# One test behind the output in place of two in the MoE; residual and first gate as identity products, second gate by token tiles

## The chip, the cores and the metric

The kernel runs on one core of one Trainium2 chip. The metric is the device time of the whole program in microseconds (us); lower is better. Before the change the median of three runs is 1718.18 us (1717.43 to 1719.94). Besides, one execution was recorded by the hardware profiler; all rows below are from it. The engines are called PE (TensorE; PEld is its weight load), DVE (VectorE), ACT (ScalarE), POOL (GpSimd) and SP (SyncE, which here issues the transfers).

## The reference

Four transformer layers run on 256 tokens of width 1024, in float32: two layers of a first kind (a mixer of three attentions, then a mixture of experts) and two of a second kind (a mixer of three branches, then a feed-forward). The change touches the mixture of experts of the first kind:

```
for i in range(2):
    ...                                                       # mixers
    h = layer_norm(ALPHA * h + mix, ln1_g[i], ln1_b[i])
    ffn = grouped_moe(h, ...)                                 # 16 experts, each token picks 2
    ple = sigmoid(h @ ple_gate[i]) * (p[i] @ ple_proj[i])
    h = layer_norm(ALPHA * h + ffn + ple, ln2_g[i], ln2_b[i])
```

`grouped_moe` gives each token two experts of one group with weights that add up to one; an expert computes `silu(h @ w_gate) * (h @ w_up) @ w_down` with 512 hidden columns.

## The kernel before

The program is first recorded as a list of operations in program order; `order` then plays a model of the engines, of the transfers and of the buffers, and writes out, for each engine, an order by earliest start, and among those that can start by place in the list (`prio`, which `prefer` and `arrange` change). Every operation is issued by one line, 554 (`call`), so groups in the profile are told apart by tile names. Engines work through their own order and wait for one another by semaphores.

Work is split into two tiles `t` of 128 tokens and column halves `n` of 512. Weights come by SP in blocks of up to 512 KB (`chunk`). Outside the experts each block `raw` is split by ACT and DVE into a high and a low part (`whi`, `wlo`) and multiplied in three passes with the split activations. Expert weights (`deep`) are used as they are, in plain fp32. `raw`, `deep`, `whi`, `wlo`, the activations `x`, `h` and the tile `r` share 43 large buffers (`big`); 128x512 work tiles share ten (`t2k`); PSUM has eight banks (`ps`).

In `moe`, a layer's mixture of experts is computed with 64 slots per expert. `r` is first set to twice the scaled residual; `ple` for the first column half multiplies the gate (`pg`) and the projection (`pp`) and adds the product to `r`. `route` picks the experts and numbers the tokens of each; `slot` is a token's place in its expert, `most` the largest number of tokens of one expert. `gather` forms the expert inputs (`xg`) by one-hot products. Then eight pairs `q` of experts follow: `gate_up` (tile `gu`), `hidden`, `down` (tiles `yh`, `yl`), and `scatter`, which adds the outputs of the pair to four PSUM banks `acc[n, t]`. In the last pair (`PLE_AT`), `ple` of the second half stands between the gate/up products and the down products, for both token tiles.

After the last scatter stands a branch: every engine loads `most` (line 561) and compares (line 562); if an expert had more than 64 tokens, `moe_rest` runs all experts densely for the tokens left over and adds to `r`. The branch has `scratch` tiles, and no operation that touches `r`, `x` or these tiles is moved across it. Then `layernorm` adds `r` at 0.5 to `acc` (`lnt`), takes the statistics, normalizes half by half and hands each half to `feat`, which transposes it (`fT`) and splits it into the next `x`. The work on the next layer's weights (`whi`, `wlo`) may start before that. At the very end SP writes the two halves of the output and waits for them.

Of the kernel before, what the change touches and what calls it, by code (L numbers as in the profile page):

```python
# [17 lines left out]
L = 2  # L18
S = 256
# [262 lines left out]
class Op:  # L282
    __slots__ = ("i", "eng", "fn", "args", "kw", "dur", "lat", "deps", "users", "new", "tiles", "epoch", "wait", "prio", "table", "cols", "body", "mode",
# [11 lines left out]
class Pool:  # L295
# [3 lines left out]
    def tile(self, shape, dtype, name, tag=None, bufs=None, cls=None):  # L299
        if self.rec.sink is not None:  # L300
            return next(self.rec.scratch[cls if cls in self.rec.scratch else tag]).bitcast(dtype)
# [6 lines left out]
BIAS_FIRST = False  # L308
MASK_GP = 0
PLE_AT = (None, 7)  # L310
# [10 lines left out]
class Recorder:  # L321


    def __init__(self, tc):
        self.tc, self.ops, self.bufs, self.sink, self.key = tc, [], {}, None, ()
        self.tensor, self.vector, self.scalar, self.gpsimd, self.sync = (
            Engine(self, n) for n in ("tensor", "vector", "scalar", "gpsimd", "sync"))

    def add(self, eng, fn, args, kw):
        if self.sink is not None:  # L330
            kw.pop("after", None)
            kw.pop("behind", None)
            self.sink.append((eng, fn, args, kw))
            return
        o = Op()
        o.i, o.eng, o.fn, o.args, o.kw, o.body = len(self.ops), eng, fn, args, kw, None
# [23 lines left out]
    def link(self, o, ins, outs):  # L360
        deps, o.tiles = set(), []
        for views, w in ((ins, False), (outs, True)):
            for v in views:
                t = v.t
                if t not in o.tiles:
# [12 lines left out]

    def branch(self, value, limit, body, scratch, behind=()):

        o = Op()
        o.i, o.eng, o.fn, o.args, o.kw = len(self.ops), "branch", "if", (value, limit), {}
        self.sink, self.scratch = [], {v[0].t.cls or v[0].t.tag: itertools.cycle(v) for v in scratch}
        body()
        o.body, self.sink = self.sink, None
        ins = [value] + [x for _, _, a, k in o.body for x in list(a) + list(k.values()) if isinstance(x, V)]
        outs = [x for _, _, a, k in o.body for x in a[:1] if isinstance(x, V)]
        self.link(o, ins, outs)
        o.deps |= set(behind)
        o.dur, o.lat, o.prio, o.nbytes, o.cols, o.table, o.mode = 2200.0, 0.0, o.i, 0, 0.0, (), None  # L390
        self.ops.append(o)


    def order(self):
# [23 lines left out]
        ready = {e: [] for e in ENGINES + ("branch",)}  # L418
# [57 lines left out]
        while len(seq) < len(ops):  # L476
# [35 lines left out]
            if o.eng == "branch":  # L512
                table = None
                for e in clock:
# [1386 lines left out]
```

## Time and profile before

| | us |
|---|---|
| median of 3 runs | 1718.18 |
| profiled execution | 1713.75 |
| its span, first to last instruction | 1711.7 |
| PE busy | 1645.6 (96%) |
| DVE busy | 902.0 (53%) |
| ACT busy | 676.2 (40%) |
| PE matmuls / DVE instructions | 8884 / 1608 |
| mean granted PE clock | 0.987 |

The span runs from the first to the last instruction; the profiled execution's own time has 2.05 us more. A busy share is that of an engine over the whole span. Waits are given as "waiting operation <- what ended the wait: us in total, times, longest". In the timeline a row is a run of equal instructions with its start and length; `x4` is their number, and what stands in brackets is the idle time before it. The MoE of layer 0 ends at about 416 us, that of layer 1 at about 810.

### The profile page before, as it was taken

The page shows a single profiled execution, that of the slowest core. Times are in us where ns is not written, and L with a number is a line of the kernel's source. Part 1 is how long each engine was busy: PE and PEld are TensorE (multiplying, and loading weights), DVE is VectorE, ACT ScalarE, POOL GpSimd, SP SyncE. Part 2 cuts the span into 40 slices and gives each one's busy share as a digit, 9 for nine tenths or more (in the row PEclk, how much of TensorE's full clock was granted, in tenths as well). Part 3 has the DMA queues.
Part 4 walks back from the last instruction along what each step waited for, and adds up shares of the span by engine and source line. Part 5 has one row for each costly group of instructions (what it writes and reads, how often), then busy time and mean ns, then how long its engine had stood idle before and what let it go on. Part 6 is the DMA issues. An engine that isn't in the chain of part 4 may idle for free.

```text
span 1711.7 us, 23099 instructions
## 1 busy us (share of the span) xinstructions
PE 1645.6 (96%) x8884; PEld 1218.5 (71%) x8884; DVE 902.0 (53%) x1608; ACT 676.2 (40%) x1032; POOL 13.0 (1%) x29
## 2 busy tenths in 40 slices
PE   6999999997999999998799999999999999999997
PEld 5887444434798544434697888899989888888996
DVE  7867211014958411103876447955587654785554
ACT  5454111113555211113454554444445454444441
POOL 1000000000000000000000000000000000000000
PEclk9999999999999999999899999999999999999999
DMA  6764899999564799999553347555645334846530
GB/s 220 272 240 153 316 409 409 409 410 371 178 233 163 275 409 409 409 409 405 205 178 132 115 159 272 196 191 185 203 157 197 127 120 148 286 171 207 193 115 25
DMA packets 117297, 414.21 MB, mean 242 GB/s; under 512 B 13250, under 2 KB 15586, under 8 KB 117172
## 3 DMA queue, kind: packets, MB, share of 16 engines
q1 hardware_dynamic: 116580, 411.35, 65.8%
q8 instruction: 73, 1.20, 0.3%
q0 software_dynamic: 592, 1.25, 0.3%
q14 instruction: 52, 0.43, 0.1%
HBM read 410.44 MB, written 2.10 MB: 241 GB/s over the span
## 4 chain that ended last, share of the span: by engine, by line
PE 49%; DVE 2%; issue 0%; ACT 0%; DVEq 0%
PE f L554 11%; PE ff L554 10%; PE gl L554 8%; PE br L554 4%; PE acc L554 3%; PE gv L554 2%; PE gq L554 1%; PE gk L554 1%; PE gg L554 1%; PE mk L554 1%; PE mv L554 1%; PE mq L554 1%; PE fT L554 1%; PE o L554 1%; PE gu L554 1%; DVE wlo L554 0%
## 5 line engine op out<-in xcount | busy, mean ns | idle before, releaser
L554 DVE TENSOR_TENSOR wlo<-raw,whi 128x1024 fp32r<-128x1024 f32 (+1 forms) x370 | 433.6, 1207 | 181.4 <-ACT whi L554 149.8
L554 ACT CAST whi<-raw 128x1024 fp32r<-128x1024 f32 (+1 forms) x370 | 369.1, 1041 | 140.7 <-PE br L554 29.0
L554 PE MATMUL gu<-deep,xg 128*64 128x512 f32 x1024 | 246.9, 597 | 4.9 <-DMA deep<-in_w_up_dram 4.5
L554 PEld LDWEIGHTS gu<-deep,xg 128*64 128x64 f32 x1024 | 76.1, 136 | 157.4 <-issue 126.9
L554 PE MATMUL ff<-whi,f 128*128 128x512 f32 x512 | 137.9, 390 | 0.0
L554 PE MATMUL y<-deep,gu 128*64 128x512 f32 x512 | 122.4, 595 | 1.7 <-DMA deep<-in_w_down_dram 1.4
L554 PE MATMUL f<-x,whi 128*128 128x256 f32 x768 | 123.4, 283 | 0.0
L554 DVE SCALAR_TENSOR_TENSOR yl<-y,gw,yh 128x512 fp32r<-128x512 f32 x32 | 24.0, 751 | 168.8 <-ACT yh L554 168.8
L554 PEld LDWEIGHTS ff<-whi,f 128*128 128x128 f32 x512 | 95.0, 188 | 19.0
L554 PEld LDWEIGHTS f<-x,whi 128*128 128x128 f32 x768 | 106.7, 192 | 0.9
L554 PE MATMUL gl<-whi,x 128*128 128x512 f32 x384 | 104.1, 391 | 0.0
L554 ACT COPY gu<-gu 128x512 f32<-128x512 f32 x32 | 18.7, 585 | 206.9 <-PE gu L554 206.9
L554 PEld LDWEIGHTS y<-deep,gu 128*64 128x64 f32 x512 | 38.9, 137 | 79.9 <-issue 67.5
L554 PEld LDWEIGHTS gl<-whi,x 128*128 128x128 f32 x384 | 71.9, 188 | 14.7
L554 PE MATMUL ff<-wlo,f 128*128 128x512 f32 x256 | 78.9, 389 | 0.0
L554 PE MATMUL f<-x,wlo 128*128 128x256 f32 x384 | 77.4, 283 | 0.0
L554 DVE TENSOR_TENSOR gu<-gu,guT 128x256 f32<-128x256 f32 x32 | 13.3, 420 | 100.8 <-ACT gu L554 100.7
L554 ACT ACTIVATE r<-r 128x512 f32<-128x512 f32 x32 | 20.3, 634 | 111.0 <-DVE r L554 111.0
L554 PE MATMUL gl<-wlo,x 128*128 128x512 f32 x192 | 60.0, 392 | 0.0
L554 PEld LDWEIGHTS f<-x,wlo 128*128 128x128 f32 x384 | 59.9, 192 | 0.0
L554 ACT ACTIVATE yh<-y,gw 128x512 fp32r<-128x512 f32 x32 | 22.0, 687 | 89.8 <-PE y L554 89.8
L554 DVE TENSOR_SCALAR r<-f 128x512 f32<-128x512 f32 x32 | 22.0, 688 | 66.7 <-PE f L554 66.5
(428 smaller groups left out, 2678.2 us busy)
## 6 DMA issues: line engine op xcount, KB each, us to landing
raw<-in_w_in_dram SPq DMA_DIRECT2D x156, 512.0 KB, 4.8
deep<-in_w_gate_dram SPq DMA_DIRECT2D x128, 512.0 KB, 10.2
deep<-in_w_up_dram SPq DMA_DIRECT2D x128, 512.0 KB, 10.2
deep<-in_w_down_dram SPq DMA_DIRECT2D x128, 512.0 KB, 10.2
raw<-in_w_ff_dram SPq DMA_DIRECT2D x128, 512.0 KB, 5.1
raw<-in_w_branch_dram SPq DMA_DIRECT2D x24, 512.0 KB, 4.7
raw<-in_w_o_dram SPq DMA_DIRECT2D x16, 512.0 KB, 5.4
raw<-in_ple_gate_dram SPq DMA_DIRECT2D x16, 512.0 KB, 6.9
```

Source lines behind the costliest of these rows:

```text
L554: getattr(getattr(self.tc.nc, eng), fn)(*[r(a) for a in args], **{k: r(v) for k, v in kw.items()})
```

## The change

The two branches in the MoE go, and `moe_rest` with them. `most` becomes a kept column per layer, and the maximum of both is stored as `many`. Behind the whole program, after the output is issued, one test of `many` follows: if any expert of either layer had more than 64 tokens, the whole program is recorded a second time (`again`) with `moe_all`, which runs all 16 experts densely, and the output is written again.

`r` goes too. The scaled residual, for the first column half together with its gate product, is kept in four 128x512 tiles (`first`) and enters `acc` by products with the identity matrix, fp32, 128x128 by 512 columns, placed in the first pair of experts; the scatters then add to it. `ple` now gives a function `gate_of(t)` for one token tile. For the second half, `gate_of(0)` stands in the last pair where both tiles stood; `gate_of(1)` is recorded after the norm of token tile 0. Its result is added to `acc[1, t]` by DVE. `layernorm` takes its two column halves as they are: `acc[0, t]` directly from PSUM, the other from `second[t]`. For the other norms the sum is now formed by `plus`.

```diff
-    def branch(self, value, limit, body, scratch, behind=()):
...
-    def run(self):
-        seq = self.order()
-        with self.tc.manual_schedule():
-            for o in seq:
-                if o.fn == "if":
-                    n = self.tc.nc.values_load(o.args[0].real(), min_val=0, max_val=S)
-                    with self.tc.If(n > o.args[1]), self.tc.manual_schedule():
-                        for c in o.body:
-                            self.call(*c)
-                else:
-                    self.call(o.eng, o.fn, o.args, o.kw)
+        for o in self.order():
...
+        self.fast = True
+
+    def again(self):
+
+        self.nc = Recorder(self.nc.tc)
+        for p in self.pools:
+            p.rec = self.nc
+        self.fast = False
 
...
-    def layernorm(self, acc, resid, lnp, hnew, x, t, alpha=ALPHA):
+    def plus(self, acc, resid, t, alpha=ALPHA):
+
+        tt = [self.t2k("lnt") for _ in range(2)]
+        for n in range(2):
+            self.nc.vector.scalar_tensor_tensor(tt[n], resid[t][:, n * 512:n * 512 + 512], alpha, acc[n], op0=OP.mult, op1=OP.add)
+        return tt
+
+    def layernorm(self, src, lnp, hnew, x, t):
 
         nc = self.nc
-        tt = [self.t2k("lnt") for _ in range(2)]
         st = self.sm(12, "st")
         for n in range(2):
-            sl = slice(n * 512, n * 512 + 512)
-            nc.vector.scalar_tensor_tensor(tt[n], resid[t][:, sl], alpha, acc[n], op0=OP.mult, op1=OP.add)
-            nc.vector.bn_stats(st[:, n * 6:n * 6 + 6], tt[n])
+            nc.vector.bn_stats(st[:, n * 6:n * 6 + 6], src[n])
         mv = self.sm(2, "mv")
         nc.vector.bn_aggr(mv, st.rearrange("p (a b) -> p a b", b=6))
         rs = self.rsqrt(mv[:, 1:2], 1e-5, 1)
         for n in range(2):
             sl = slice(n * 512, n * 512 + 512)
-            nc.vector.scalar_tensor_tensor(tt[n], tt[n], mv[:, 0:1], lnp[0][:, sl],
-                                           op0=OP.subtract, op1=OP.mult)
-            nc.vector.scalar_tensor_tensor(hnew[t][:, sl], tt[n], rs, lnp[1][:, sl],
-                                           op0=OP.mult, op1=OP.add)
+            tt = self.t2k("lnt") if src[n].t.space == PS else src[n]
+            nc.vector.scalar_tensor_tensor(tt, src[n], mv[:, 0:1], lnp[0][:, sl], op0=OP.subtract, op1=OP.mult)
+            nc.vector.scalar_tensor_tensor(hnew[t][:, sl], tt, rs, lnp[1][:, sl], op0=OP.mult, op1=OP.add)
             if x is not None:
...
+
+    def slots(self, l, pick):
+
+        nc = self.nc
         p = self.ps("pos")
...
-        most = self.small.tile([128, 1], I32, name=self.nm("most"), tag="most", bufs=2)
-        nc.vector.tensor_reduce(most, p[:, 32:48], axis=AX.X, op=OP.max)
-        return gate, slot, most
-
-    def moe_rest(self, l, x, gr, r):
+        nc.vector.tensor_reduce(self.most[:, l:l + 1], p[:, 32:48], axis=AX.X, op=OP.max)
+        if l == L - 1:
+            nc.vector.tensor_reduce(self.many, self.most, axis=AX.X, op=OP.max)
+        return slot
+
+    def moe_all(self, l, h, x):
 
...
-    def ple(self, l, x, px, r, n):
+    def ple(self, l, x, px, n):
 
         nc, A = self.nc, self.A
         wp = self.wblock(A["ple_proj"], l * 256 * D + n * 256 * 512, 2, 512, PLE_CLS)
         pp = []
         for p in self.toks("pp", px, wp):
             a = self.t2k("pp")
-            nc.scalar.copy(a, p)
+            nc.scalar.activation(a, p, AF.Copy, scale=0.5)
             pp.append(a)
         w = self.wblock(A["ple_gate"], l * D * D + n * D * 512, 8, 512, PLE_CLS)
-        for t, p in enumerate(self.toks("pg", x, w)):
+
+        def gate_of(t):
+            p = self.ps("pg", "dense")
+            self.stream((w, [((t,), self.tok(p, x, t))]))
             a = self.t2k("pg")
             nc.scalar.activation(a, p, AF.Tanh, scale=0.5)
             nc.vector.scalar_tensor_tensor(a, a, 1.0, pp[t], op0=OP.add, op1=OP.mult)
-            sl = slice(n * 512, n * 512 + 512)
-            nc.vector.tensor_add(r[t][:, sl], r[t][:, sl], a)
-
-    def moe(self, l, h, x, cap=CAP):
+            return a
+
+        return pp, gate_of
+
+    def moe(self, l, h, x):
+
         nc, A = self.nc, self.A
-        r = self.htile("r")
+        i = len(nc.ops)
+        first = [[], []]
+        _, gate_of = self.ple(l, x, self.load_p(l), 0)
         for t in range(2):
-            nc.scalar.activation(r[t], h[t], AF.Copy, scale=2.0 * ALPHA)
-        i = len(nc.ops)
-        for n in range(2):
-            if PLE_AT[n] is None:
-                self.ple(l, x, self.load_p(l), r, n)
+            a = gate_of(t)
+            nc.vector.scalar_tensor_tensor(a, h[t][:, 0:512], ALPHA, a, op0=OP.mult, op1=OP.add)
+            first[0].append(a)
+            a = self.t2k("ah")
+            nc.scalar.activation(a, h[t][:, 512:1024], AF.Copy, scale=ALPHA)
+            first[1].append(a)
         k = len(nc.ops)
         ht = XT([self.x4("hth", (128, 1024)) for _ in range(2)], [self.x4("htl", (128, 1024)) for _ in range(2)])
         for t in range(2):
             nc.scalar.copy(ht.hi[t], h[t])
             nc.vector.tensor_sub(ht.lo[t], h[t], ht.hi[t])
-        gate, slot, most = self.route(x)
-        gr = self.sm(32, "grest")
-        nc.vector.scalar_tensor_tensor(gr, slot, float(cap), gate, op0=OP.is_gt, op1=OP.mult)
-        if cap < CAP:
-            nc.vector.scalar_tensor_tensor(slot, slot, float(cap), slot, op0=OP.is_le, op1=OP.mult)
+        gate, pick = self.route(x)
+        slot = self.slots(l, pick)
...
-                        nc.tensor.matmul(acc[n, t], ST[q][:, t * 128:(t + 1) * 128], ys[n][i], start=q == 0 and i == 0,
+                        nc.tensor.matmul(acc[n, t], ST[q][:, t * 128:(t + 1) * 128], ys[n][i], start=False,
                                          stop=q == NE // 2 - 1 and i == 1, behind=behind)
...
                 scatter(q - 1, ys, whole)
+            else:
+                for t in range(2):
+                    for n in range(2):
+                        nc.tensor.matmul(acc[n, t], self.ident, first[n][t], start=True, stop=False, behind=whole)
             hid.append(hidden(b[0]))
             if q < 7:
                 a = gate_up(2 * q + 2)[0]
-            for n in range(2):
-                if q == PLE_AT[n]:
-                    self.ple(l, x, self.load_p(l), r, n)
+            else:
+                _, gate_of = self.ple(l, x, self.load_p(l), 1)
+                second = [gate_of(0)]
             ys = down(q, hid)
             if q < 7:
                 b = gate_up(2 * q + 3)
         scatter(7, ys)
-        scratch = [[self.ring_tile("raw")], [self.ring_tile("whi")], [self.ring_tile("wlo")],
-                   [self.t2k("rest") for _ in range(6)], [self.ps("rest") for _ in range(2)]]
-        nc.branch(most[0:1, 0:1], cap, lambda: self.moe_rest(l, x, gr, r), scratch, [len(nc.ops) - 1])
-        return r, acc
-
-    def block1(self, l, h, x, w0=None, cap=CAP):
+
+        def sums(t):
+            if t:
+                second.append(gate_of(t))
+            nc.vector.tensor_add(second[t], second[t], acc[1, t])
+            return acc[0, t], second[t]
+
+        return sums
+
+    def block1(self, l, h, x, w0=None):
         mixT = self.mixers1(l, x, w0)
         hn, x1 = self.wo_ln(l, h, mixT)
-        r, acc = self.moe(l, hn, x1, cap)
+        if self.fast:
+            sums = self.moe(l, hn, x1)
+        else:
+            r = self.moe_all(l, hn, x1)
+            sums = lambda t: [r[t][:, n * 512:n * 512 + 512] for n in range(2)]
         lnp = self.load_lnp(2 * l + 1)
         h2 = self.htile("h2")
         x2 = self.xT("x2")
         for t in range(2):
-            self.layernorm([acc[0, t], acc[1, t]], r, lnp, h2, x2, t, alpha=0.5)
...
         m = Model(tc, A, ctx)
...
+
+        def program():
+            x = m.xT("x")
+            w0 = m.wblock(A["w_in"], 0, 8, W1_BLOCKS[0][1])
+            if m.fast:
+                m.load_bias()
+            for i, c in enumerate(w0):
+                m.load_x(x, i)
+                c()
+            if m.fast:
+                m.setup()
+            h = None
+            for l in range(L):
+                h, x = m.block1(l, h, x, None if l else w0)
+            for l in range(L):
+                h, x = m.block2(l, h, x, l == L - 1)
+            for t in range(2):
+                m.nc.sync.dma_start(out[0, t * 128:(t + 1) * 128], h[t])
+            m.nc.run()
+
+        with tc.manual_schedule():
+            program()
+
+            n = tc.nc.values_load(m.many[0:1, 0:1].real(), min_val=0, max_val=S)
+            with tc.If(n > CAP), tc.manual_schedule():
+                m.again()
+                program()
```

## Rows read from the trace of the kernel before

**Rows 1.** Waits of PE and DVE, 409 to 430, then 805 to 824.
```profile
PE fT L554 <- DVE h L554: 13.1, 1, 13.1
DVE lnt L554 <- DVEq L562: 6.0, 1, 6.0
...
PE fT L554 <- DVE h L554: 12.8, 2, 12.5
DVE lnt L554 <- PEq L562: 5.7, 1, 5.7
```

**Rows 2.** Windows: us, busy PE, PEld, DVE, ACT, POOL, PEclk, DMA share, GB/s.
```profile
416.20:422.80 6.60, 0.01 (x1) 0.00 (x0) 0.64 (x1) 0.90 (x2) 0.00 (x0) 0.76 1.02 391
422.80:429.30 6.50, 0.00 (x0) 0.01 (x1) 6.01 (x17) 2.49 (x4) 0.00 (x0) 0.50 0.28 107
```

**Rows 3.** Timeline, layer 0: start, us, engine, line, operation [idle before].
```profile
401.29 1.07 PE L554 MATMUL pg<-whi,x 128*128 128x512 f32 x4
...
406.82 7.09 PE L554 MATMUL y<-deep,gu 128*64 128x512 f32 x32
...
414.68 0.75 DVE L554 SCALAR_TENSOR_TENSOR yl<-y,gw,yh 128x512 fp32r<-128x512 f32 x1 [0.27 <-ACT yh L554]
...
415.48 0.73 PE L554 MATMUL acc<-yl,oh 128*128 128x512 f32 x2
...
422.84 0.69 DVE L554 SCALAR_TENSOR_TENSOR lnt<-r,acc 128x512 f32<-128x512 f32 x1 [6.00 <-DVEq L562]
...
424.17 0.67 DVE L554 SCALAR_TENSOR_TENSOR lnt<-r,acc 128x512 f32<-128x512 f32 x1
...
429.32 1.09 PE L554 MATMUL fT<-const,h 128*128 128x128 f32 x4 [13.10 <-DVE h L554]
```

**Rows 4.** Lines 561 and 562: ns min/median/max, first and last start us.
```profile
L561 SPq TENSOR_LOAD <-most x2: 473/480/487, 415.9 to 810.0; - x2
...
L562 SPq EVENT_SEMAPHORE  x16: 17/17/17, 422.7 to 821.0; - x16
L562 POOLq COMPARE_BRANCH  x2: 45/49/53, 176.2 to 810.1; - x2
...
L562 PEldq COMPARE_BRANCH  x2: 6128/6150/6172, 416.1 to 809.6; - x2
```

**Rows 5.** Timeline of SP, then the DMA issues' us to landing, 380 to 430.
```profile
388.39 7.76 SPq L554 DMA_DIRECT2D deep<-in_w_down_dram  x8
...
deep<-in_w_down_dram SPq DMA_DIRECT2D x8, 512.0 KB, 8.7
```

**Rows 6.** Groups by form: busy us, mean ns, idle before.
```profile
L554 DVE SCALAR_TENSOR_TENSOR lnt<-lnt,mv,lnp 128x512 f32<-128x512 f32 x32 | 23.9, 746 | 0.0
...
L554 DVE SCALAR_TENSOR_TENSOR pg<-pg,pp 128x512 f32<-128x512 f32 x8 | 5.5, 690 | 17.6 <-ACT pg L554 17.6
```

**Rows 7.** Timeline of DVE and of PE, 444 to 468.
```profile
453.13 2.35 DVE L554 TENSOR_TENSOR wlo<-raw,whi 128x1024 fp32r<-128x1024 f32 x2
...
455.72 1.04 PE L554 MATMUL dv<-wlo,x 128*128 128x512 f32 x2
```

**Rows 8.** Waits of PE's weight loads, 300 to 390, then 700 to 790.
```profile
PEld gu L554 <- DMA deep<-in_w_up_dram: 12.8, 12, 1.7
...
PEld gu L554 <- DMA deep<-in_w_up_dram: 12.1, 12, 1.1
```

**Rows 9.** Waits of SP, 170 to 190; then SP's timeline.
```profile
SPq L554 <- PE gu L554: 12.8, 4, 10.2
...
358.35 9.28 SPq L554 DMA_DIRECT2D deep<-in_w_down_dram  x8
```

**Rows 10.** Timeline of SP at the end; the output's rows: ns; us to landing.
```profile
1697.17 11.21 SPq L554 DMA_DIRECT2D out_dram<-h  x2
...
L554 SPq DMA_DIRECT2D out_dram<-h x2: 343/344/344, 1697.2 to 1708.0; - x2
DMA to landing us min/median/max: 2.6/2.7/2.7
```

More of the change, by code (lines that the diff above doesn't have):

```diff
@@ L282 @@
 class Op:
-    __slots__ = ("i", "eng", "fn", "args", "kw", "dur", "lat", "deps", "users", "new", "tiles", "epoch", "wait", "prio", "table", "cols", "body", "mode",
+    __slots__ = ("i", "eng", "fn", "args", "kw", "dur", "lat", "deps", "users", "new", "tiles", "epoch", "wait", "prio", "table", "cols", "mode",
                  "nbytes", "key")
@@ L329, in add @@
     def add(self, eng, fn, args, kw):
[L330 to L334, printed above, removed]
         o = Op()
-        o.i, o.eng, o.fn, o.args, o.kw, o.body = len(self.ops), eng, fn, args, kw, None
+        o.i, o.eng, o.fn, o.args, o.kw = len(self.ops), eng, fn, args, kw
         after, behind = kw.pop("after", []), kw.pop("behind", ())
@@ L364, in link @@
                 t = v.t
+                if t.rec is not self:
+                    t.rec, t.acc, t.left, self.bufs[t.key] = self, [], 0, t.bufs
                 if t not in o.tiles:
@@ L417, in order @@
         dma, table, cols, mode = 0.0, None, {}, None
-        ready = {e: [] for e in ENGINES + ("branch",)}
+        ready = {e: [] for e in ENGINES}
         rtime = [0.0] * len(ops)
@@ L511, in order @@
             end = s + dur
-            if o.eng == "branch":
-                table = None
-                for e in clock:
-                    clock[e] = max(clock[e], s) + o.dur
-                best_of.clear()
-            else:
-                clock[o.eng] = end
+            clock[o.eng] = end
             if o.nbytes:
@@ L1302, in wo_ln @@
         for t in range(2):
-            self.layernorm([acc[0, t], acc[1, t]], h, lnp, hn, x1, t)
+            self.layernorm(self.plus([acc[0, t], acc[1, t]], h, t), lnp, hn, x1, t)
         return hn, x1
@@ L1823, in block2 @@
         for t in range(2):
-            self.layernorm([acc[0, t], acc[1, t]], h, lnp, hn, x1, t)
+            self.layernorm(self.plus([acc[0, t], acc[1, t]], h, t), lnp, hn, x1, t)
         lnp = self.load_lnp(5 + 2 * l)
@@ L1862, in block2 @@
         for t in range(2):
-            self.layernorm([acc[0, t], acc[1, t]], hn, lnp, h2, x2, t)
+            self.layernorm(self.plus([acc[0, t], acc[1, t]], hn, t), lnp, h2, x2, t)
         return h2, x2
```

68 lines of the change are left out of this document (26 added, 42 removed).

## The prediction

> **What bounds the kernel now.** On the page TensorE (PE) is busy nearly throughout, so what is to be had lies in the few stretches where it stands still. The table of waits, read next, names them: the transposes after the layer norm that closes each MoE wait 13.1 us in layer 0 and 12.5 us in layer 1 for VectorE (DVE) [rows 1]. The table by windows shows what else happens there [rows 2]: PE is empty, its granted clock falls to 0.50, and the DMA engines, full in the first half, fall to 0.28 in the second.
>
> The timeline gives the order in layer 0 [rows 3]: the down products of the last pair of experts until 413.9, the last scatter from 415.48, DVE's first layer-norm instruction at 422.84, the first transpose at 429.32. DVE's own wait is 6.0 us, and 5.7 us in layer 1, put down to the branch [rows 1]. The rows of the branch explain it [rows 4]: every engine loads the count, compares and jumps over the body; PE's compare-and-branch takes 6.13 us, and SyncE (SP), which loads at 415.9, goes on at 422.7. GpSimd (POOL), which has no work in the body, spends 49 ns. So the price is that of a far jump. The other half of the stall is the DVE chain of the norm, 422.84 to 429.32, beside which PE has nothing to do.
>
> By the Trainium skill (Runtime: NRT & Kernel Launch, Instruction fetch mechanics) a taken branch whose target is not in the fetched window stops the engine for a fetch. The trace agrees: 6.13 us on PE against 49 ns on POOL [rows 4]. By that rule the fetch is not removed but moved to the program's end.
>
> **The change part by part.** The profiled execution took 1713.75 us, span 1711.7 and 2.05 around it; the runs' median is 1718.18, so 4.43 goes on top at the end.
>
> *The two branches go, and the gate of token tile 1 moves behind the scatter.* The gate product of one token tile is 24 matmuls, from 401.29 until the down products at 406.82 [rows 3], 5.4 us with the small wait ahead of these taken off. Without it the down products start at about 401.4. Their last weights are issued at 395.8 and land 8.7 us later, 404.5 [rows 5]; PE asks for the last pair after six eighths of its 7.09 us, at 406.7, so it does not wait. The scatter ends near 410.8 instead of 416.2, and PE does the 24 matmuls until 416.2 while DVE does the norm of tile 0. That chain is 5.15 us from the second `lnt` (424.17) to the transpose (429.32), and the new addition to `acc[1,0]` stands where that `lnt` stood: transposes at about 416.1. PE would have no gap; the upper bound of the gain is 13.1 us in layer 0 and 12.5 in layer 1.
>
> But then DVE is late next. From the first conversion of the next weights until both tiles of `x` are split, DVE has one long pause, the branch [rows 1]. In the new order it has the same work less this: the pause, 6.0; two `yl` of 0.75, which come 5.4 us earlier with the down products and fall ahead of the stretch, 1.5; and four `lnt` of 0.68 against two additions and one gate instruction of 0.69 [rows 3, 6], 0.65. That is 8.15 us; in layer 1, if one `yl` is counted, 5.7 + 0.75 + 0.65 = 7.1. After it PE feeds on weights that DVE splits: the first of the two chunks begun at 453.13 is ready at about 454.3 (half of 2.35 us) and PE's next products with split weights start at 455.72 [rows 7], a margin of 1.4 us. I take the lower end plus that margin, 9.5 and 8.5, because these rows are nearer to the new state than the empty PE: together -18.0, bounds -15.2 and -25.6.
>
> *Four identity products per layer.* A fp32 product of 512 columns is two passes; 32 passes in 7.09 us, two side by side in the halves of the array [rows 3], make 0.44 per pass, 0.89 per product, 3.5 us a layer and 7.1 in all. They stand early, beside the first pair of experts. Later in the MoE PE's weight loads wait for `up` weights alone for 12.8 us in layer 0 (300 to 390) and 12.1 in layer 1 (700 to 790) [rows 8]. So the 3.5 us are taken from later waits: 0. If that cover were gone, +7.1.
>
> *The tile `r` goes.* It held two of the 43 large buffers through the MoE. Before the first gate product SP waits up to 10.2 us for a buffer that PE frees (layer 0, and layer 1 is built alike); two more buffers let two more transfers start there, and the MoE, which transfers pace to its end, finishes up to 2 x 1.28 us earlier (eight issues in 9.28 us, seven steps [rows 9]). Against it: `h` is now held until the gate of its second tile, and the planner may give the room to something else. Bounds 0 and -5.1; I take the middle, -2.6, as SP's row shows the want of room but nothing of the planner.
>
> *Cost nothing:* the scaling of `h` and the additions to `r` were ScalarE and DVE work beside PE's gate products, and as many of the same length replace them; `plus` and `layernorm` together have the old instructions; the weights of the second gate are loaded at the same place in SP's queue; the norm now reads `acc[0,t]` from PSUM twice.
>
> On that last point the trace has 0.67 to 0.69 us with a PSUM operand and 746 ns for the same operation from SBUF with a pointer more [rows 3, 6]: no penalty. The Trainium skill (VectorE: DVE Perf Modes, Rules for kernel authors) offers to copy a matmul's output from PSUM to SBUF first if many operations follow; by it the second reading would count against the change, by the rows it does not.
>
> *The test at the end.* SP issues the last output from 1708.04 to 1708.38, and it lands 2.7 us after the start [rows 10]. Now a load and the jump are queued behind that issue on SP, and nothing waits behind them but the end. From the load at 415.9 to the first step after the jump at 422.7 were 6.8 us, and eight semaphore steps of 17 ns follow (16 in two branches) [rows 4]; the landing passes beside it: 6.8 + 0.1 - 2.4 = +4.5. The transfers that shared the queues then (1.02 [rows 2]) are absent at the end, which may shorten it; a jump like POOL's would make it 0. If the landing were only waited for behind the jump, it would be +6.9. I stay near the far jumps: +4.5.
>
> Sum: -18.0 - 2.6 + 0 + 4.5 = -16.1; 1713.75 - 16.1 = 1697.6, plus 4.4: **1702 us** for the median.
>
> **Rivals.** (a) *PE gets the whole stall back.* The planner finds other matmuls (the key and query blocks) while DVE splits weights, so 25.6 + 5.1 - 4.5 = 26.2 come off: 1692. For: PE's rows at 455.72 show no wait in brackets. Against: the margin of 1.4 us [rows 7].
>
> (b) *The second gate half does not end up behind the scatter*, because the planner fills expected waits for down weights with it. Then the scatter ends as before, PE stands empty beside the norm, and only the branch and the saved DVE instructions come off: 6.0 + 5.7 + 1.3 - 4.5 = 8.5: 1710. For: these matmuls are ready early. Against: the down weights were there when PE came [rows 3, 5].
>
> (c) *The identity products are not hidden*, because the transfers follow PE's releases of buffers all along, and the spare buffers bring nothing: -15.2 + 7.1 + 4.5 = -3.6: 1715. Against: [rows 8].
>
> (d) *Slower: the small buffers run out.* Ten 128x512 buffers serve everything. Four are now parked from the first gate until the identity products, through routing, gather and the first gate/up copies. If the first gate product has to wait for one, the delay is passed on whole, because transfers wait for that product [rows 9]. From 9.8 us a layer on ((16.1 + 3.4) / 2) the kernel is slower; at 12 us it takes 1718.2 - 16.1 + 24 = 1726. Against: the parked tiles follow `pg` tiles that were needed until just before the gather anyway.
>
> That the dense pass runs is excluded: both branches of the trace skipped their bodies, and the limit of 64 is the same.
>
> **How the numbers follow.** The forecast has 0.54, with its own range 1697 to 1709; (a) 0.20, (b) 0.13, (c) 0.07, (d) 0.06. About 0.2% (3.4 us) is what a measurement can tell from no change, so faster is below 1714.8: the forecast, (a), (b) and half of (c), 0.90; within 0.2% the rest of (c) and the edge of (d), 0.05; slower 0.05. The range 1691 to 1713 leaves out nearly half of (a) and all of (c) and (d), and takes in the bounds of the stall, the buffers and the end.
>
> **What would show it.** Right: DVE starts the norm within 1 us of the last scatter; the 24 gate matmuls lie between that scatter and the first transpose, and PE's wait there is under 2 us; short waits of PE for split weights turn up in the 30 us after it; the last gate/up product ends at the same time or 1 to 3 us earlier; some 5 us lie between the landing of the output and the end. Wrong: gate matmuls ahead of the down products (b), a MoE that ends 3 us later (c), a late first gate product (d), or a jump at the end that takes under 2 us.

## The result and the profile after

The changed kernel takes 1700.42 us in the median of four runs (1697.73 to 1705.73), beside 1718.54 us of the kernel before, measured with it; the ratio is 0.9898, 95% interval 0.9872 to 0.9924. Measured again beside the experiments it was 0.9883, 0.9864 to 0.9902. The profiled execution took 1699.02 us, span 1696.8, mean clock 0.990.

The page has PE as busy as before in us, in a shorter span, so what went is PE's idle time:

```profile
span 1696.8 us, 23084 instructions
PE 1646.7 (97%) x8900; PEld 1223.8 (72%) x8900; DVE 896.3 (53%) x1599; ACT 675.4 (40%) x1032; POOL 13.0 (1%) x29
```

PE's timeline at the end of the MoE of layer 0 answers to [rows 3]. Each row is a run of equal instructions with start and length, and in brackets the idle time before it:

```profile
383.42 1.93 PE L528 MATMUL gu<-deep,xg 128*64 128x512 f32 x6 [0.21 <-DMA deep<-in_w_up_dram]
...
396.37 7.09 PE L528 MATMUL y<-deep,gu 128*64 128x512 f32 x32
...
404.89 1.07 PE L528 MATMUL pg<-whi,x 128*128 128x512 f32 x4
405.80 0.62 PE L528 MATMUL acc<-yl,oh 128*128 128x512 f32 x2
...
411.29 0.66 PE L528 MATMUL fT<-const,h 128*128 128x128 f32 x4 [0.35 <-DVE h L528]
413.05 0.43 PE L528 MATMUL mla<-whi,x 128*128 128x352 f32 x1 [1.10 <-ACT x L528]
...
415.61 0.80 PE L528 MATMUL mla<-whi,x 128*128 128x352 f32 x4
420.70 0.66 PE L528 MATMUL fT<-const,h 128*128 128x128 f32 x4 [4.29 <-DVE h L528]
422.15 1.11 PE L528 MATMUL fT<-const,h 128*128 128x128 f32 x4 [0.79 <-DVE h L528]
```

The down products start 10.4 us earlier, the last scatter at 405.8 instead of 415.5, and the gate of token tile 1 lies behind it, until the transposes, which wait 0.35 us instead of 13.1. But the transposes of tile 1 now wait 4.29 us. Layer 1 shows the same, and its table of waits (columns: waiting operation <- what ended it, us in total, times, longest) answers to [rows 1]:

```profile
PE fT L528 <- DVE h L528: 5.6, 3, 4.3
PE gv L528 <- ACT x L528: 0.7, 1, 0.7
```

DVE has no pause there. Its timeline in layer 0, and two rows of ACT and SP:

```profile
400.79 0.75 DVE L528 SCALAR_TENSOR_TENSOR yl<-y,gw,yh 128x512 fp32r<-128x512 f32 x1 [3.00 <-ACT yh L528]
404.16 0.70 DVE L528 BATCH_NORM_STATS2 st<-acc 128x6 f32<-128x512 f32 x1 [2.62 <-PE acc L528]
...
411.94 0.75 DVE L528 SCALAR_TENSOR_TENSOR h<-pg,rz,lnp 128x512 f32<-128x512 f32 x1
...
414.24 0.89 DVE L528 TENSOR_TENSOR wlo<-raw,whi 128x704 fp32r<-128x704 f32 x1
...
421.34 0.75 DVE L528 SCALAR_TENSOR_TENSOR h<-pg,rz,lnp 128x512 f32<-128x512 f32 x1
422.01 0.88 DVE L528 TENSOR_TENSOR wlo<-raw,whi 128x704 fp32r<-128x704 f32 x1
...
424.21 0.68 DVE L528 TENSOR_TENSOR x<-fT,x 128x512 fp32r<-128x512 f32 x1
...
404.53 3.48 ACT L528 CAST whi<-raw 128x704 fp32r<-128x704 f32 x4 [0.34 <-DMA raw<-in_w_in_dram]
...
394.69 5.45 SPq L528 DMA_DIRECT2D raw<-in_w_in_dram  x5
```

The next mixer's first weights land at 404.5, when the norm of tile 0 begins. DVE then does that norm, one conversion, the norm of tile 1, and only behind it the other conversions. PE multiplies nothing from 416.4 to 420.7.

At the end of the program, the first step after the jump stands where [rows 4] had it behind the branch (columns: count, shortest, median and longest ns, first and last start):

```profile
L1904 POOLq COMPARE_BRANCH  x1: 53/53/53, 1219.3 to 1219.3; - x1
L1904 PEldq COMPARE_BRANCH  x1: 4010/4010/4010, 1679.7 to 1679.7; - x1
L1904 SPq COMPARE_BRANCH  x1: 50/50/50, 1691.1 to 1691.1; - x1
L1904 SPq EVENT_SEMAPHORE  x8: 17/17/17, 1693.8 to 1694.3; - x8
```

SP compares at 1691.1 and goes on at 1693.8. DVE's last instruction ends at 1689.8, and 7.0 us pass from there to the end of the span, 3.7 before.

The span by stages, in us, one profiled execution of each kernel, from the start or end times of the instructions named (the runs below the line are the experiments; "again" is the changed kernel once more):

```
                     A     MoE 0  end 0  MoE 1  end 1  rest   tail   span
before              37.5   233.3   89.0  231.6   87.5  838.0   3.7  1711.7
changed             37.1   228.6   82.1  229.0   84.1  838.0   7.0  1696.8
---
changed, again      37.2   228.8   83.2  229.4   81.9  838.1   7.0  1696.4
no_test             41.0   230.0   82.5  229.5   84.6  837.7   3.6  1700.8
gate_back           43.3   228.7   82.6  229.1   83.1  838.5   6.9  1702.4
two_held            37.0   232.0   82.7  233.3   83.9  837.8   7.5  1704.2
ident_twice         36.9   231.3   82.5  231.8   83.8  838.8   7.2  1702.8
ident_late          42.5   228.3   84.7  229.4   82.6  836.6   7.6  1701.7
no_branch           43.2   233.2   84.2  232.6   83.1  838.1   3.6  1709.3
pool_low            40.4   228.9   82.6  230.8   83.3  838.3   6.6  1700.8
pool_one_operand    36.8   228.6   80.4  229.2   84.0  839.6   7.1  1695.8
pool_two            36.8   228.5   80.6  229.9   81.0  838.1   6.4  1691.4
early_load          36.4   228.5   82.4  229.6   83.0  839.1   7.2  1697.1
```

A runs from the last `sbv` products of layer 0 to the first router product; "MoE" from the first router product to the last gate/up product of the layer; "end 0" from there to the last `dk` product of the next mixer, "end 1" to the first `gq` product; "rest" from there to the last `h`; "tail" from the last DVE instruction to the end. What lies ahead of A (118 to 120 us) and between "end 0" and MoE 1 (71.5 to 71.7) is left out. The same order of work differs from one execution to another by 4 to 6 us in A, up to 1.4 in MoE 0, and 1 to 2.7 at the ends.

### The profile page after: what moved, and what is told of

Same layout as the page of the kernel before. It is cut to its first block, busy times and chain, and to the rows that moved or that the text cites. A ratio compares the mean times of both kernels' runs of the same rounds, so it can differ in the third digit from the quotient of the medians.

```text
span 1696.8 us, 23084 instructions
## 1 busy us (share of the span) xinstructions
PE 1646.7 (97%) x8900; PEld 1223.8 (72%) x8900; DVE 896.3 (53%) x1599; ACT 675.4 (40%) x1032; POOL 13.0 (1%) x29
## 4 chain that ended last, share of the span: by engine, by line
PE 84%; DMA 8%; DVE 6%; ACT 1%; issue 1%; SPq 0%; DVEq 0%
PE gu L528 11%; PE f L528 11%; PE ff L528 10%; PE gl L528 8%; PE acc L528 7%; PE y L528 4%; PE br L528 4%; DMA deep<-in_w_up_dram 4%; DMA deep<-in_w_down_dram 3%; PE gv L528 2%; PE xg L528 2%; PE pg L528 2%; PE gk L528 1%; PE dk L528 1%; PE gq L528 1%; PE dq L528 1%
## 5 line engine op out<-in xcount | busy, mean ns | idle before, releaser
L528 PE MATMUL gu<-deep,xg 128*64 128x512 f32 x1024 | 236.9, 596 | 2.6 <-DMA deep<-in_w_up_dram 2.2
```

Of the source, the lines that this page charges most:

```text
L528: getattr(getattr(self.tc.nc, o.eng), o.fn)(*[r(a) for a in o.args], **{k: r(v) for k, v in o.kw.items()})
```

## Experiments

**The test at the end, by itself** (no_test):

```diff
-            n = tc.nc.values_load(m.many[0:1, 0:1].real(), min_val=0, max_val=S)
-            with tc.If(n > CAP), tc.manual_schedule():
-                m.again()
-                program()
```

> The changed kernel without the test at the end (the dense pass is left out with it). The two traces put the stretch from the last DVE instruction to the last instruction at 6.6 us or so with the test and 3.4 us before. If the test costs what it adds there, the span is 3.3 us shorter than the changed kernel's (1696.8 to about 1693.5), the stretch is 3.4 to 3.7 us, and nothing ahead of it moves. The prediction's price would make it 4.5 us shorter. If the landing of the output hides the jump, the difference is under 1 us.

The tail is 3.6 us, with the test 7.0: 3.4 us, as the theory had it. The rest of the expectation was missed: the span is 4.0 us longer, not 3.3 shorter, and the median was 1702.86 (ratio to before 0.9911, 0.9894 to 0.9929), no faster than with the test. The profiled execution lost 4 us in A and 1.3 in MoE 0, which have the same instructions in the same order. So the price of 3.4 us is read from the stage, and the whole time does not show it.

**The moved gate product** (gate_back):

```diff
-                second = [gate_of(0)]
+                second = [gate_of(0), gate_of(1)]
...
-            if t:
-                second.append(gate_of(t))
```

> The changed kernel with the gate of token tile 1 back in the last pair, ahead of the down products. Theory: what the move gains at the scatter (5.4 us a layer) is mostly given back, since the weights of the next mixer land only 5 us earlier and DVE then splits them behind the norms; with the gate back, DVE has time to split them ahead of the norm, PE's wait for the transposes of tile 1 (4.3 us) goes, and a wait of 5 to 6 us for those of tile 0 comes. So it is 0 to 3 us a layer slower, 1697 to 1703 as a span. Rival, the price of the prediction's case (b): the move is worth 5 us a layer, the kernel is 8 to 11 us slower than the changed one, and the wait of tile 1 stays as it is.

1699.12 us, ratio 0.9881, 0.9860 to 0.9903: not slower at all. Both ends together take 165.7 us, against 166.2 and 165.1 in the two executions of the changed kernel, so the move is worth nothing that stands out from what two executions differ by. The rival, 8 to 11 us, is out. The reason is in the rows, DVE first and then PE (the times are some 5 us later than in the changed kernel, since A took 6 us more):

```profile
410.74 0.89 DVE L528 TENSOR_TENSOR wlo<-raw,whi 128x704 fp32r<-128x704 f32 x1 [2.13 <-ACT whi L528]
...
412.27 2.50 DVE L528 TENSOR_TENSOR wlo<-raw,whi 128x704 fp32r<-128x704 f32 x3
...
421.45 1.12 PE L528 MATMUL fT<-const,h 128*128 128x128 f32 x4 [4.87 <-DVE h L528]
...
429.62 0.66 PE L528 MATMUL fT<-const,h 128*128 128x128 f32 x4
```

With the last scatter ending 25.8 us behind the last gate/up product instead of 21.1, the four chunks are there and split ahead of the norm, which starts at 415.70. PE waits 4.87 us for tile 0 and not at all for tile 1; with the move it is 0.35 and 4.29.

**The buffers of `r`** (two_held):

```diff
+        held = self.htile("held")
+        for t in range(2):
+            nc.scalar.activation(held[t], h[t], AF.Copy, scale=ALPHA)
...
+            nc.vector.tensor_copy(self.sm(1, "rel"), held[t][:, 0:1])
```

> The changed kernel with two large buffers written when the MoE starts and read behind its last scatter, as the tile r held them. Theory: in the changed kernel the transfers of each MoE are 2.6 us earlier for two more buffers, and in layer 0 another 2 us for an earlier first gate product. With the two held, the last gate/up product of each layer comes 2 to 3 us later than in the changed kernel, and the span is 2 to 5 us longer (the stretch behind may take some back). Rival: the lead comes from the earlier first product and the identity products' place alone, and the last gate/up products stay within 0.5 us.

MoE 0 takes 232.0 us and MoE 1 233.3, that is 3.3 and 4.1 more than the means of the changed kernel's two executions (228.7, 229.2), and the median rises to 1706.07 (ratio 0.9942, 0.9921 to 0.9963). The theory holds, with more than its 2 to 3 us. The delay does not come at the start, where the edit adds two ScalarE instructions: the down products of the fifth pair begin 153.3 us behind the first router product of layer 0 in both kernels, those of the sixth 184.9 instead of 181.6. PE's weight loads wait again for `up` weights, for 11.9 us in layer 0 as they did before for 12.8 [rows 8]; here the run with two held first, then the changed kernel:

```profile
PEld gu L528 <- DMA deep<-in_w_up_dram: 11.9, 13, 1.1
```

```profile
PEld gu L528 <- DMA deep<-in_w_up_dram: 7.7, 8, 1.3
```

**The identity products doubled** (ident_twice; the operands halved):

```diff
...
-                        nc.tensor.matmul(acc[n, t], self.ident, first[n][t], start=True, stop=False, behind=whole)
+                        for i in range(2):
+                            nc.tensor.matmul(acc[n, t], self.ident, first[n][t], start=i == 0, stop=False, behind=whole)
```

> The changed kernel with each of the four identity products issued twice per layer (the four operands halved, so the sums are the same): 3.5 us more of PE work per layer early in the MoE. Theory: PE waits for up and down weights later in the MoE (7.7 + 3.6 us in layer 0 of the changed kernel), so the last gate/up products come within 0.5 us of where they are and the span changes by less than 1 us. Rival (the prediction's case c): they are not hidden, and the last gate/up products are 3.5 us later in each layer, the span 7 us longer.

Both MoE are 2.6 us longer; the ratio is 0.9922 (0.9905 to 0.9939). So four further products are not hidden, against the theory: they put PE 3.4 us back early, SP's waits for buffers that the gate/up products free rise from 19.4 to 25.3 us in layer 0, and 2.6 us remain at the end. What the first four cost was left to the next run.

**The identity products late** (ident_late):

```diff
-                        nc.tensor.matmul(acc[n, t], ST[q][:, t * 128:(t + 1) * 128], ys[n][i], start=False,
+                        nc.tensor.matmul(acc[n, t], ST[q][:, t * 128:(t + 1) * 128], ys[n][i], start=q == 0 and i == 0,
...
-            else:
+            if q == 5:
...
-                        nc.tensor.matmul(acc[n, t], self.ident, first[n][t], start=True, stop=False, behind=whole)
+                        nc.tensor.matmul(acc[n, t], self.ident, first[n][t], start=False, stop=False, behind=whole)
```

> The changed kernel with the four identity products in the sixth pair of experts instead of the first. In the run with eight products a layer the four added ones delayed PE by 3.4 us early and the end of the MoE by 2.7 us. Theory: early in the MoE PE's pace sets when buffers come free and so the transfers; late in it transfers set the pace. Placed late, the products cost nothing, transfers run 2 to 3 us earlier, and each MoE ends 2 to 3 us earlier: 4 to 6 us in all. Rival (the prediction's case d): four of the ten small buffers held through five pairs hold up the copies of the expert products, and the MoE ends later, not earlier.

PE was 3.1 us further at the first down products and 2.3 at the fifth, but the MoE took 228.3 and 229.4 us, within 0.5 us of the early products; the ratio is 0.9884 (0.9866 to 0.9902). The theory's gain did not come, and the rival's loss neither. At its late place the 3.4 us are taken up at once: in layer 0 the sixth pair's down products come 3.1 us later than in the changed kernel, the seventh's 0.2. At the early place they cost the same within 0.5 us. No run left them out; but two_held, which holds the buffers as before, takes 465.3 us for both MoE against 464.9 before, so the products and all else that changed in the MoE come to 0.4 together (-1.3 and +1.7 by layer). The cover ends little behind them, as ident_twice shows.

**The branches alone** (no_branch: the kernel before without them):

```diff
-        nc.branch(most[0:1, 0:1], cap, lambda: self.moe_rest(l, x, gr, r), scratch, [len(nc.ops) - 1])
```

> The kernel before with its two branches taken out and nothing else (the dense pass is left out with them). Theory: a branch costs what it keeps DVE from, 6 us a layer, and its removal brings nearly all of that, since the weights of the next mixer are still split ahead of the norm: the transposes come 6 us after the last scatter's end instead of 13, the wait of PE for those of tile 1 stays under 0.5 us, and the kernel is 10 to 13 us faster than before. With the test at the end (3.4 us by the run without it) that would leave 7 to 10 of the changed kernel's 15 to 18 us to the branches. Rival: without the branch the planner reorders the stretch and PE gets back the whole 13 us, 25 us in all. Second rival: it is hidden by work that is late anyway, under 5 us.

1710.11 us against 1719.02, ratio 0.9943 (0.9930 to 0.9956): 8.9 us. The ends are 4.8 and 4.4 us shorter, the MoE 0.1 shorter and 1.0 longer. That is a little under the theory's 10 to 13, and both rivals are out. The transposes wait 5.49 us instead of 13.1, for the norm alone:

```profile
427.33 1.11 PE L554 MATMUL fT<-const,h 128*128 128x128 f32 x4 [5.49 <-DVE h L554]
```

**DVE's conversions on POOL** (pool_low):

```diff
...
-        nc.vector.tensor_sub(lo[:, :w], raw[:, :w], hi[:, :w])
+        (nc.gpsimd if self.low and self.low.pop() else nc.vector).tensor_sub(lo[:, :w], raw[:, :w], hi[:, :w])
...
                 h, x = m.block1(l, h, x, None if l else w0)
+                m.low = [m.fast] * 4
```

> The changed kernel with the low parts of the four chunks of the first weight block behind each MoE computed by POOL instead of DVE (3.5 us of DVE work in layer 0, 4.9 in layer 1). Theory: DVE is what PE waits for there; the transposes of tile 1 come 1 us earlier in layer 0, and the split weights are there when PE comes back, so PE's products of that stretch end 1 to 3 us earlier a layer, 2 to 6 us in all. Rival: POOL's subtractions are too long (over 3 us each) or slow DVE down while both run, and the stretch ends at the same time or later.

The wait for tile 1 was gone, as the theory said, but the norm of tile 0 came 3 and 6.7 us later, and the ends were as long as before this edit (ratio 0.9899, 0.9880 to 0.9919). The rival's second half is what happened. DVE in layer 1, then POOL:

```profile
797.38 0.15 DVE L528 TENSOR_SCALAR rz<-ri 128x1 int32<-128x1 int32 x1
797.57 1.70 DVE L528 SCALAR_TENSOR_TENSOR ra<-rz,rx 128x1 f32<-128x1 f32 x1
799.30 1.21 DVE L528 SCALAR_TENSOR_TENSOR rz<-ra,rz 128x1 f32<-128x1 f32 x1
800.54 2.27 DVE L528 SCALAR_TENSOR_TENSOR ra<-rz,rx 128x1 f32<-128x1 f32 x1
802.84 2.26 DVE L528 SCALAR_TENSOR_TENSOR rz<-ra,rz 128x1 f32<-128x1 f32 x1
805.14 0.22 DVE L528 SCALAR_TENSOR_TENSOR ra<-rz,rx 128x1 f32<-128x1 f32 x1
...
794.47 4.77 POOL L528 TENSOR_TENSOR wlo<-raw,whi 128x1024 fp32r<-128x1024 f32 x2 [379.86 <-DMA raw<-in_w_in_dram]
799.18 1.30 POOL L528 TENSOR_TENSOR wsT<-wsT,const 128x512 f32<-128x512 f32 x1
800.41 4.67 POOL L528 TENSOR_TENSOR wlo<-raw,whi 128x1024 fp32r<-128x1024 f32 x2
```

A Newton step (one of the small instructions on 128x1 elements that compute the norm's reciprocal root) lasts until POOL's instruction ends, and 0.22 us right after: the steps end at 799.27, 800.51 and 805.10, POOL's instructions at 799.24, 800.48 and 805.08. A tensor_scalar beside POOL takes 0.15 us.

**The same with one tensor operand, and with two chunks** (pool_one_operand, pool_two):

```diff
...
-                nc.vector.scalar_tensor_tensor(a, z, x, z, op0=OP.mult, op1=OP.mult)
+                nc.vector.tensor_scalar(a, z, x, z, op0=OP.mult, op1=OP.mult)
...
+                nc.vector.tensor_scalar(z2, a, -k, z, op0=OP.add, op1=OP.mult)
...
-                m.low = [m.fast] * 4
+                m.low = [m.fast] * 2
```

The last pair of lines is pool_two alone.

> The changed kernel with POOL computing the low parts of the four chunks behind each MoE, as in the run before, and the six Newton steps of the norms' reciprocal root written as tensor_scalar with two 128x1 scalars (one tensor operand) in place of scalar_tensor_tensor (two). In the run before, such steps took 1.2 to 2.3 us instead of 0.2 whenever POOL was subtracting, while DVE instructions with one operand from SBUF beside them kept their times; that delayed the norm of tile 0 by 2.9 and 6.7 us. Theory: DVE instructions with two SBUF operands are held up by POOL's; then the steps take 0.2 us again, the transposes of tile 0 wait under 2 us, those of tile 1 under 2 us too, and each layer's stretch is 2 to 4 us shorter than in the changed kernel. Rival: small operands or pointers are what is held up; then the norm is as late as in the run before.

> The same with POOL computing the low parts of two chunks only behind each MoE, and DVE the other two. Theory (two SBUF operands are held up): POOL ends before the long steps of the norm of tile 0 begin (3.4 us of work in layer 0, 4.8 in layer 1), so nothing is held up, DVE has two conversions less, and the stretch is 1 to 3 us shorter than in the changed kernel, less than with all four if those hold up nothing, more if they do. Rival: the wait for tile 1 stays at 4.3 us, since the norm of tile 1 has no conversion ahead of it but one, and the stretch is within 1 us.

With four chunks on POOL (median 1696.65, ratio 0.9869, 0.9847 to 0.9892) the steps are short again, and the next instruction with two operands from SBUF is the one held up, in layer 1 for as long as POOL works:

```profile
790.02 0.27 DVE L528 TENSOR_SCALAR ra<-rz,rx 128x1 f32<-128x1 f32 x1
...
791.58 0.74 DVE L528 SCALAR_TENSOR_TENSOR lnt<-acc,mv,lnp 128x512 f32<-128x512 f32 x1
792.36 1.16 DVE L528 SCALAR_TENSOR_TENSOR h<-lnt,rz,lnp 128x512 f32<-128x512 f32 x1
793.44 2.85 DVE L528 SCALAR_TENSOR_TENSOR pg<-pg,mv,lnp 128x512 f32<-128x512 f32 x1
796.33 2.71 DVE L528 SCALAR_TENSOR_TENSOR h<-pg,rz,lnp 128x512 f32<-128x512 f32 x1
```

`lnt`, with one of its two operands in PSUM, keeps its 0.74 us. The theory of two operands from SBUF holds, the rival of small operands falls; the gain of 2 to 4 us came in layer 0 only (80.4 us). With two chunks POOL is done in time in both layers, the ends take 80.6 and 81.0 us, 4.0 less together than the changed kernel's mean (165.6), and the longest wait for a transpose is 2.8 us in layer 0 and 1.9 in layer 1. This is the best version run: 1695.67 us, ratio 0.9867 (0.9846 to 0.9889). The steps as tensor_scalar alone do not explain it: with them and nothing on POOL (early_load, below) the ends take 165.4 us. But the interval overlaps that of the changed kernel, whose ends differ by 1.1 and 2.2 us from one execution to the next, so that pool_two beats it rests on the stages of one execution and is likely, not shown.

By the Trainium skill (SBUF — State Buffer, Who interferes with whom) a DVE instruction with two inputs in SBUF contends with a GpSimd instruction that reads SBUF, over a read interface that both share as an exclusive lock. The trace agrees: `pg<-pg,mv,lnp` takes 2.85 us beside POOL, against 0.75 without at 806.12 of the same execution.

**The count loaded early** (early_load; Newton steps as above, nothing on POOL):

```diff
...
-        for o in self.order():
+        for i, o in enumerate(self.order()):
+            if i == at:
+                hook()
...
-            m.nc.run()
-
+            m.nc.run(len(m.nc.ops) - 600 if m.fast else None, lambda: n.append(tc.nc.values_load(m.many[0:1, 0:1].real(), min_val=0, max_val=S)))
...
-            with tc.If(n > CAP), tc.manual_schedule():
+            with tc.If(n[0] > CAP), tc.manual_schedule():
```

> The changed kernel with the Newton steps as tensor_scalar and nothing on POOL, and with the count loaded into the engines' registers in the middle of the last layer instead of behind the output; the compare and jump stay at the end. Theory: at the end SP's load (0.5 us and the steps around it, 1690.2 to 1691.1) leaves the path, the fetch of 2.6 us stays: the stretch from the last DVE instruction to the end is 6.0 to 6.2 us instead of 7.0; the norms behind the MoE are up to 0.3 us shorter. Rival: the loads make the engines wait for one another where they now stand, and the last layer is longer by more than the end saves.

A miss: the tail is 7.2 us. SP compares 0.8 us earlier and goes on no earlier:

```profile
L1909 SPq COMPARE_BRANCH  x1: 50/50/50, 1690.3 to 1690.3; - x1
L1909 SPq EVENT_SEMAPHORE  x8: 17/17/17, 1693.9 to 1694.4; - x8
```

So the jump takes 3.6 us instead of 2.7. It may wait behind the output's transfer: in all ten profiles with the test SP goes on 3.9 to 4.1 us behind the issue of that transfer, whether it compares 1.3 us behind it or, here, 0.4, and always behind its landing (3.0 to 3.5 us). No run moved the transfer, so this is not shown. The rival's loss cannot be told either: the rest takes 839.1 us, within what the other runs show (836.6 to 839.6). Ratio 0.9909 (0.9890 to 0.9927).

**The changed kernel again**:

> The changed kernel once more, beside the others of this call, to see what of the stages' times repeats. Expected: the last gate/up products, the scatters and the transposes at the same distances from each other as in its first profile within 0.5 us, except where the granted clock falls at another moment (the output products of the first mixer, 119 to 156 us, took 4.5 us more in two of the kernels that have the same order there).

1698.13 us, ratio 0.9883 (0.9864 to 0.9902). Its stages are in the table: all within 0.5 us but the two ends, which differ by 1.1 and 2.2, more than the 0.5 expected.

## Why the prediction was right or wrong

The time was right (1702 forecast, 1700.4 measured), and the likeliest case is what happened in kind. Its terms were not: two large errors cancel, so that the sum came out near is luck. On the profiled executions, before to changed (and to its second execution):

```
term                                forecast   measured
branches, moved gate (both ends)     -18.0     -10.4   (-11.4)
two buffers of r (both MoE)           -2.6      -7.3    (-6.7)
identity products                      0        0 (within the MoE)
test at the end                       +4.5      +3.3    (+3.3)
stage A and the rest                   0        -0.5    (-0.5)
sum                                  -16.1     -14.9   (-15.3)
```

*Branches and moved gate: the mis-sized term, outside its bounds of -15.2 and -25.6.* The steps up to the transposes came as worked out: the gate's 5.4 us at the scatter, no gap at the transposes, DVE late next. The step that failed is the lower bound: the prediction took the end of DVE's stretch, with both tiles of `x` split, for the end of the loss. DVE's stretch did end earlier, and by more than the 8.15 and 7.1 us of the forecast: `x` is split 39.5 us behind the last gate/up product instead of 51.4 in layer 0, 40.8 instead of 51.9 in layer 1. But it does not have "the same work less this". Before, four chunks were split between 410 and 415, while PE was at down products and scatters:

```profile
410.33 0.89 DVE L554 TENSOR_TENSOR wlo<-raw,whi 128x704 fp32r<-128x704 f32 x1 [1.36 <-ACT whi L554]
...
411.91 2.49 DVE L554 TENSOR_TENSOR wlo<-raw,whi 128x704 fp32r<-128x704 f32 x3
...
441.05 0.69 DVE L554 TENSOR_TENSOR x<-fT,x 128x512 fp32r<-128x512 f32 x1
...
399.70 5.45 SPq L554 DMA_DIRECT2D raw<-in_w_in_dram  x5
...
438.19 0.66 PE L554 MATMUL fT<-const,h 128*128 128x128 f32 x4 [0.43 <-DVE h L554]
```

The weights come with the transfers, which moved by 5 us only, the scatter by 10. So conversions fell behind the norms, three of the four behind both. And PE, not DVE, sets the end: before, PE had 6 us of products with split weights between the two tiles' transposes; in the changed kernel it has 3, and what it does not do there it does afterwards. From its last transposes to the first `dk` product it works for 29.8 us instead of 24.8, with no wait over 0.6 in either; 2.9 of the 29.8 are at the lower of the clock's two levels (1.2 GHz; granted 0.50 until 425.0), to which it fell after the 4.29 us without work. The right sum is PE's idle time: 13.1 us [rows 1] and two waits of 0.4 against 0.35 + 1.10 + 4.29 + 0.79 = 6.5 in layer 0, a gain of 7.4 for 6.9 measured. The runs divide the term: the branches bring 9.2 (no_branch), the moved gate nothing (gate_back). The 1.6 that gate_back has over no_branch may lie in what else changed around the norm; it is no more than two executions differ by.

In layer 1 PE's waits for the transposes and for `x` fall by 6.7 us (13.0 to 6.3), the end by 3.4, and in the second execution by 5.6. Some of the gain goes back in a lower clock there too: after the 4.29 us without work the granted clock is 0.52 of full speed for 6.6 us, mostly the lower level. Before, it was at that level for 3.4 us of work behind the stall (822.4 to 825.8, 0.50); the first execution of the changed kernel has it once more from 838.0 to 841.4 (0.50), the second does not (1.00). The windows of that layer, columns as in [rows 2]:

```profile
796.20:804.40 8.20, 3.24 (x17) 2.32 (x17) 7.75 (x20) 4.74 (x7) 0.00 (x0) 0.97 1.03 406
804.40:811.00 6.60, 6.27 (x19) 4.96 (x20) 6.57 (x8) 4.26 (x5) 0.00 (x0) 0.52 0.24 92
```

*The buffers: mis-sized the other way, outside its bounds of 0 and -5.1.* The prediction took half of two transfers a layer; two_held gives 3.3 and 4.1 us, more than the 2.56 of two whole transfers, and together (7.4) all of the MoE's gain. The step that failed is the bound of two transfers, gained once before the first gate product: in layer 0 two_held falls behind between the fifth and the sixth pair. Why it is more than two transfers is not settled.

*The identity products: 0, right within what was measured, by a narrow margin.* PE's later waits, the reason given, do not cover much more: 3.4 us more cost 2.6 (ident_twice).

*The test at the end:* +3.3 for +4.5, and this too from two errors. The jump is shorter than in the MoE: SP needs 3.6 us from its load to the next step instead of 6.8, PE's compare 4.0 instead of 6.13 [rows 4]. The queues moved 27 GB/s in the last slice of the page, a reason that the prediction had named as possible. The output landed beside the jump, as forecast, so this alone would give +1.3. The other 2.0 us come behind the jump and were not in the sum: 3.1 us from SP's first step to the end, where before 1.1 passed from the landing to the end. Nineteen semaphore steps of SP take 1.3 of them, and a pause of 0.8 follows, whose cause is not shown. POOL's compare took 53 ns again.

*The 4.43 us for the median* were too much: the changed kernel's median stands 1.4 above its profile. The profile of before was a short execution (its runs reach from 1712.7 to 1725.3), which is why the medians differ by more (18 us) than the profiles (14.7).

Rival (a) is refuted: PE got back 10.4 of the 25.6 us, and no other matmuls filled the wait for tile 1. (b) did not happen and would have cost nothing: with the gate put back the time is the same. (c) and (d) did not occur. Of the signs, "short waits of PE for split weights" was wrong: there is one wait of 4.29 us, for the second norm. The last gate/up product came 4.7 us earlier in layer 0, outside the 1 to 3 (2.6 in layer 1), and 3.5 us lie between the landing of the output and the end, not 5.

## What to carry to other kernels

Price a stall by the idle time of the bound engine before and after, through to the point where its queue is full again, and ask for every operand of that stretch when it arrives in the new order; an edit that ends a stage earlier does not make the next stage's weights land earlier. Before moving work into a gap, look at what the helper engine did in that gap: here DVE split weights there, and the move brought nothing. Where transfers pace a stage, buffers held through it are dear (3 to 4 us for two of 43), while 3.4 us of matmuls can be free and the next 3.4 cost 2.6.

## What was not expected of the hardware

- POOL's subtraction (1.7 us for 128x704, 2.4 for 128x1024) stops DVE instructions that read two operands from SBUF until it ends, even on 128x1 elements (2.27 us for 0.22); those with one operand in PSUM (0.74 us), bn_stats (0.69) and tensor_scalar (0.27) run on.
- Stage A took 36 to 38 us in some executions and 40 to 43 in others, in the same order of work. The granted clock tells them apart: full in the changed kernel, 0.73 on average in gate_back, where it is at the lower level (1.2 GHz) for 10 us. Ahead of it PE stands still for DVE (`doT` <- `o`): 2.3 us in gate_back, 0.9 to 1.9 in the other long ones, up to 1.0 in the short ones. What makes that wait longer is not shown. The windows, the changed kernel first, then gate_back:

```profile
119.00:137.00 18.00, 17.18 (x82) 12.70 (x81) 12.37 (x38) 14.57 (x25) 0.00 (x0) 1.00 0.14 46
```

```profile
118.00:137.00 19.00, 16.67 (x62) 12.46 (x61) 11.81 (x41) 12.30 (x21) 0.00 (x0) 0.73 0.15 48
```

- A jump over a large body cost more behind the MoE (6.13 us on PE, 5.9 on SP from compare to next step) than at the end of the program (4.0 on PE, 2.7 on SP). The bodies differ, and the cause is not shown.
